# Input projection with 512-column matmuls for the high weights, ACT drains and an accumulating DMA

## The chip, the cores and the metric

The kernel runs on one core of one Trainium2 chip. The metric is the device time of one execution in microseconds; before the change it was 1963.8 us in the median of three runs (1961.78 to 1964.49). Five engines matter: PE multiplies matrices, DVE and ACT work elementwise (both read PE's result banks), POOL works elementwise between buffers of the on-chip memory, SP only issues transfers (DMAs). Each engine works off its own queue in order; between engines there are only semaphores.

## The reference, cut to what matters

The whole is a two-layer trunk in float32 over 512 positions of width 2048. The change touches one matrix product of the first layer, `h @ w_in`, 512 × 2048 by 2048 × 8192:

```python
def pool_mixer_layer(x, norm_g, w_in, w_group, scale, w_out):
    B, S, _ = x.shape
    h = rmsnorm(x, norm_g)
    proj = h @ w_in
    u, gate = proj[..., :W_A], proj[..., W_A:]
    ...
    y = y * jax.nn.silu(gate)
    return x + y @ w_out
```

Pooling over time, a product per group, the gate and an output product follow; then a shared key/value side, 16 heads of attention with a block-causal mask, and a last output product.

## The kernel before

Everything lies transposed: 128 channels on the partitions, 512 positions along a row. PE multiplies in a rounded 32-bit format. So that little precision is lost, each operand is split into a rounded high part and the low rest, and a product is three matmuls: high weight by high x, high weight by low x, low weight by high x.

The kernel is written for a framework that turns it into one instruction list for each engine: it allots buffers and adds semaphores, and orders the instructions by a timeline that it reckons beforehand. The order on each engine can therefore differ from the order of the text, but is fixed once built.

The input projection (lines 259 to 409) saves products with a scheme that does 2 × 2 blocks with seven products in place of eight. The blocks are two k-tiles of 128 (`2j`, `2j+1`), two output tiles (`pair`), and two halves of the positions, H = 256. There are NJ = 8 k-pairs `j`. The steps:

- An opening loop over `j` (lines 353 to 374) loads x, scales it with the norm's gain (`x_parts`, line 272), forms the seven combinations of x and splits them into `xh[j]` and `xl[j]`, which stay resident (`x_sums`, line 286). In the same loop four output tiles are computed without the scheme, to keep PE busy.
- Then come 30 pairs, in the order 18 to 31 and 0 to 15 (line 396), each with four rounds q of two k-pairs. In a round `w_combos` (line 294) loads the weights of the two output tiles into a `raw` buffer (three exist) with two DMAs of SP, forms four sums (two by one DVE addition, line 301; two by POOL, lines 303 and 304), has ACT round all seven into `hi` (line 307) and DVE subtract for `lo` (line 308). `hi` and `lo` have two buffers each.
- `seven` (line 318) issues the seven products of a k-pair, three matmuls of 256 columns each (lines 324, 326, 328). The seven sums of a pair lie in the halves of four banks, and there are two such sets (`banks`, line 311).
- `gather` (line 331) combines the seven sums into four blocks `e` straight out of the banks: one ACT copy (line 334) and four DVE additions (lines 335 to 338). The results go to scratch in HBM (line 347); pairs 0 to 3 pass through the first pooling beforehand (line 345).
- Beside the first pairs the squares of x for the norm are summed up (`square`, line 387): a load, an ACT square, a DVE addition each.

What comes after (pooling, the products of line 140 to 142 with 512 columns each, attention) is not changed.

Of the kernel before, what the change touches and what calls it, by code (L numbers as in the profile page):

```python
# [7 lines left out]
F32 = mybir.dt.float32  # L8
# [6 lines left out]
P = 128  # L15
S = 512
# [35 lines left out]
def trunk_kernel(  # L52
# [206 lines left out]
    with ExitStack() as c1:  # L259
        xcp = c1.enter_context(tc.tile_pool(name="xcp", bufs=NJ))  # L260
        w7 = c1.enter_context(tc.tile_pool(name="w7", bufs=2, **tile_))
        ps7 = c1.enter_context(tc.tile_pool(name="ps7", bufs=2, space=bass.MemoryType.PSUM))
        xh, xl = [None] * NJ, [None] * NJ

        def x_load(j):

# [4 lines left out]

        def x_parts(j, c, hp):

            h = xcp.tile([P, 7, H], F32R, tag="xh", name="xh")
            lo = xcp.tile([P, 7, H], F32R, tag="xl", name="xl")
            xh[j], xl[j] = h, lo
            h12 = hp.tile([P, H], F32R, tag="h12", name="h12", bufs=NJ)
            l12 = hp.tile([P, H], F32R, tag="l12", name="l12", bufs=NJ)
            A.activation(c[:, 2:8:5, :], c[:, 2:8:5, :], AF.Copy, scale=cs[:, C_GA + 2 * j:C_GA + 2 * j + 1])
            A.activation(c[:, 0:2, :], c[:, 0:2, :], AF.Copy, scale=cs[:, C_GA + 2 * j + 1:C_GA + 2 * j + 2])  # L280
            A.copy(h[:, 0:3, :], c[:, 0:3, :])
            V.tensor_tensor(lo[:, 0:3, :], c[:, 0:3, :], f(h[:, 0:3, :]), ALU.subtract)
            split(c[:, 7, :], h12, l12)
            return h12, l12

        def x_sums(j, c):
            h, lo = xh[j], xl[j]
            V.tensor_tensor(c[:, 3:5, :], c[:, 1:3, :], c[:, 7:8, :].broadcast_to([P, 2, H]), ALU.subtract)
            V.scalar_tensor_tensor(c[:, 5, :], c[:, 4, :], -1.0, c[:, 1, :], ALU.mult, ALU.subtract)
            V.scalar_tensor_tensor(c[:, 6, :], c[:, 5, :], -1.0, c[:, 0, :], ALU.mult, ALU.subtract)  # L290
            A.copy(h[:, 3:7, :], c[:, 3:7, :])
            V.tensor_tensor(lo[:, 3:7, :], c[:, 3:7, :], f(h[:, 3:7, :]), ALU.subtract)

        def w_combos(pair, q):

            c = w7.tile([P, 2, 8, P], F32, tag="raw", name="raw", bufs=3)
            for m in range(2):
                nc.sync.dma_start(c[:, :, 2 - 2 * m:4 - 2 * m, :],
                                  awin[2 * pair + m][:, q * S:(q + 1) * S].rearrange(
                                      "p (j k n) -> p j k n", j=2, k=2))  # L300
            V.tensor_tensor(c[:, :, 4:6, :], c[:, :, 0:1, :].broadcast_to([P, 2, 2, P]),  # L301
                            c[:, :, 1:3, :], ALU.add)
            G.tensor_tensor(c[:, :, 6, :], c[:, :, 4, :], c[:, :, 2, :], ALU.add)  # L303
            G.tensor_tensor(c[:, :, 7, :], c[:, :, 6, :], c[:, :, 3, :], ALU.add)
            hi = w7.tile([P, 2, 7, P], F32R, tag="hi", name="hi")
            lo = w7.tile([P, 2, 7, P], F32R, tag="lo", name="lo")
            A.copy(hi, c[:, :, 1:8, :])  # L307
            V.tensor_tensor(lo, c[:, :, 1:8, :], f(hi), ALU.subtract)  # L308
            return hi, lo

        def banks():
            return [ps7.tile([P, 2, H], F32, tag=f"k{i}", name=f"k{i}") for i in range(4)]


        SEVEN = ((2, 0, 0, 0), (0, 6, 1, 0), (1, 2, 2, 0), (3, 4, 3, 0),
                 (5, 5, 0, 1), (6, 1, 1, 1), (4, 3, 2, 1))

        def seven(ks, w, j):
            hi, lo = w
            for wi, xi, b, h in SEVEN:  # L320
                dst = ks[b][:, h, :]
                first, last = j == 0 and h == 0, j == NJ - 1

                T.matmul(dst, hi[:, j % 2, wi, :], xh[j][:, xi, :], start=first, stop=False,  # L324
                         skip_group_check=True)
                T.matmul(dst, hi[:, j % 2, wi, :], xl[j][:, xi, :], start=False, stop=False,  # L326
                         skip_group_check=True)
                T.matmul(dst, lo[:, j % 2, wi, :], xh[j][:, xi, :], start=False, stop=last,  # L328
                         skip_group_check=True)

        def gather(ks, pair):

            e = epool.tile([P, 7, H], F32, tag="e", name="e")
            A.copy(e[:, 6, :], ks[2][:, 0, :])
            V.tensor_tensor(e[:, 0:2, :], e[:, 6:7, :].broadcast_to([P, 2, H]), ks[0], ALU.add)
            V.tensor_tensor(e[:, 2, :], e[:, 1, :], ks[2][:, 1, :], ALU.add)
            V.tensor_tensor(e[:, 3:6:2, :], e[:, 1:3, :], ks[3][:, 0:1, :].broadcast_to([P, 2, H]), ALU.add)
            V.tensor_tensor(e[:, 4:7:2, :], e[:, 2:4, :], ks[1], ALU.add)
            for i, v in enumerate((e[:, 0:7:6, :], e[:, 4:6, :])):
# [10 lines left out]
        accs = [ps7.tile([P, 2, H], F32, tag=f"k{i}", name=f"k{i}") for i in range(4)]  # L350
        with ExitStack() as c2:
            hp = c2.enter_context(tc.tile_pool(name="hp", bufs=2, **tile_))
            for j in range(NJ):
# [11 lines left out]
                a, b = xh[j], xl[j]  # L365
# [11 lines left out]
        for o in range(0, 4, 2):  # L377
            e = epool.tile([P, 7, H], F32, tag="e", name="e")
            for i in range(2):
                v = e[:, 2 * i:2 * i + 2, :]  # L380
                A.copy(v, accs[o + i])
                raws[32 + o + i] = dram()
                nc.sync.dma_start(raws[32 + o + i].rearrange("p (h t) -> p h t", h=2), v)

        sq = [tt_(), tt_()]

# [7 lines left out]
                V.tensor_tensor(sq[k % 2], sq[k % 2], x, ALU.add)  # L394

        for n, pair in enumerate((*range(18, 32), *range(16))):
            ks = banks()
            for q in range(NJ // 2):
                w = w_combos(pair, q)
                seven(ks, w, 2 * q)  # L400
                seven(ks, w, 2 * q + 1)
            if n < 8:
                square(2 * n)
                square(2 * n + 1)
            if n == 8:
                V.tensor_tensor(sq[0], sq[0], sq[1], ALU.add)
                p = ps7.tile([P, 2, H], F32, tag="k3", name="k3").rearrange("p h t -> p (h t)")
# [528 lines left out]
```

## Time and profile before

| what | value |
|---|---|
| median of three runs | 1963.8 us |
| the profiled execution, whole | 1961.67 us |
| its span, first to last instruction | 1959.9 us |
| mean granted PE clock | 0.999 |
| ACT, DVE and POOL busy from 436 to 660 us | 78.3, 149.2, 71.2 of 224 us |
| mean DMA rate over the span | 120 GB/s |

A row of a group reads: line, engine, operation, written tile <- read tiles, shape, count | busy time, mean ns of one | idle time of the engine just before them, and what ended it. A row of the timeline begins with the start and the duration in microseconds. A matmul's duration there is longer than its share of PE's time, because matmuls are pipelined; the distance from one start to the next is what the stream pays. "k" are the banks of the input projection, "mm" those of the later products. The windows give busy time per engine in a stretch, then the granted clock, the mean busy share of the 16 DMA engines and GB/s. SPq is the queue of SP, from which the transfers are issued.

### The profile page before, as it was taken

To read this page: it belongs to the slowest core of one execution; us is meant where nothing else is said; L and a number is where in the kernel's file an instruction comes from. 1 tells how busy PE (TensorE), PEld (TensorE's weight loads), DVE (VectorE), ACT (ScalarE), POOL (GpSimd) and SP (SyncE) were. 2 spreads that over 40 slices of the span, in tenths; PEclk is the share of its full clock that TensorE was granted. 3 is DMA by queue.
4 is the path that set the end of the run, shared out by engine and by line. 5 is a ranking of instruction groups with operands and counts; after the bars stand their busy time and mean duration, and the time that the engine had idled before them with its cause. 6 is when DMAs were issued, how large, how long until landed. Compare 5 with 4: busy or idle time off the path is not lost.

```text
span 1959.9 us, 30545 instructions
## 1 busy us (share of the span) xinstructions
PE 1933.3 (99%) x11324; PEld 1707.0 (87%) x11324; DVE 1280.2 (65%) x2305; ACT 815.1 (42%) x1553; POOL 262.9 (13%) x404
## 2 busy tenths in 40 slices
PE   8999999999999999999999999999999999999999
PEld 7899999999999888888888888888888888878887
DVE  8766676797666587485694567573345888786432
ACT  7533333333333443333323454332245677774221
POOL 0432332334332100000000000000010111210000
PEclk9999999999999999999999999999999999999999
DMA  6644344435444464344344343233332111111632
GB/s 198 201 135 138 119 140 130 129 120 173 140 128 132 162 205 148 113 124 140 118 126 139 113 145 123 87 97 97 97 92 75 46 38 59 52 58 46 217 119 86
DMA packets 168134, 235.51 MB, mean 120 GB/s; under 512 B 14897, under 2 KB 95153, under 8 KB 167985
## 3 DMA queue, kind: packets, MB, share of 16 engines
q1 hardware_dynamic: 167696, 233.37, 37.9%
q8 instruction: 88, 1.44, 0.3%
q14 instruction: 62, 0.50, 0.1%
q10 hardware_dynamic: 288, 0.20, 0.0%
HBM read 208.35 MB, written 25.17 MB: 119 GB/s over the span
## 4 chain that ended last, share of the span: by engine, by line
PE 93%; DVE 3%; DMA 2%; issue 1%; ACT 1%; SPq 0%; DVEq 0%; ACTq 0%
PE mm L142 16%; PE mm L140 16%; PE mm L141 16%; PE k L328 9%; PE k L324 9%; PE k L326 9%; PE sc L728 3%; PE mm L604 1%; PE mm L602 1%; PE mm L603 1%; PE tr L687 1%; PE mm L622 1%; PE mm L624 1%; PE mm L623 1%; DVE lo L308 1%
## 5 line engine op out<-in xcount | busy, mean ns | idle before, releaser
L122 ACT CAST whi<-raw 128x512 fp32r<-128x512 f32 (+2 forms) x421 | 255.7, 611 | 518.9 <-PE mm L141 455.7
L324 PE MATMUL k<-xh,hi 128*128 128x256 f32 x1680 | 460.1, 283 | 0.1
L326 PE MATMUL k<-xl,hi 128*128 128x256 f32 x1680 | 460.0, 283 | 0.0
L123 DVE TENSOR_TENSOR wlo<-raw,whi 128x512 fp32r<-128x512 f32 (+2 forms) x421 | 281.9, 672 | 222.2 <-ACT whi L122 217.8
L328 PE MATMUL k<-xh,lo 128*128 128x256 f32 x1680 | 418.1, 284 | 3.9 <-DVE lo L308 3.9
L307 ACT CAST hi<-raw 128x1792 fp32r<-128x1792 f32 x120 | 202.8, 1690 | 373.5 <-PE k L328 258.2
L308 DVE TENSOR_TENSOR lo<-raw,hi 128x1792 fp32r<-128x1792 f32 x120 | 248.9, 2074 | 158.5 <-ACT hi L307 158.5
L142 PE MATMUL mm<-bt,wlo 128*128 128x512 f32 x860 | 335.3, 390 | 0.0
L140 PE MATMUL mm<-bt,whi 128*128 128x512 f32 x860 | 334.6, 389 | 0.0
L141 PE MATMUL mm<-bt,whi 128*128 128x512 f32 x860 | 334.4, 389 | 0.0
L324 PEld LDWEIGHTS k<-xh,hi 128*128 128x128 f32 x1680 | 322.5, 192 | 0.3 <-ACT hi L307 0.3
L326 PEld LDWEIGHTS k<-xl,hi 128*128 128x128 f32 x1680 | 322.5, 192 | 0.0
L328 PEld LDWEIGHTS k<-xh,lo 128*128 128x128 f32 x1680 | 296.7, 192 | 5.6 <-DVE lo L308 5.1
L140 PE MATMUL mm<-at,whi 128*128 128x512 f32 x516 | 201.7, 392 | 3.1 <-ACT whi L122 3.1
L142 PE MATMUL mm<-at,wlo 128*128 128x512 f32 x516 | 202.0, 392 | 2.2 <-DVE wlo L123 2.2
L141 PE MATMUL mm<-at,whi 128*128 128x512 f32 x516 | 201.8, 391 | 0.0
L142 PEld LDWEIGHTS mm<-bt,wlo 128*128 128x128 f32 x860 | 161.4, 188 | 34.3 <-issue 0.5
L140 PEld LDWEIGHTS mm<-bt,whi 128*128 128x128 f32 x860 | 161.4, 188 | 33.8 <-ACT whi L122 0.2
L141 PEld LDWEIGHTS mm<-bt,whi 128*128 128x128 f32 x860 | 161.4, 188 | 33.3
L303 POOL TENSOR_TENSOR raw<-raw 128x256 f32<-128x256 f32 x120 | 101.3, 844 | 437.3 <-DVE raw L301 414.7
L142 PEld LDWEIGHTS mm<-at,wlo 128*128 128x128 f32 x516 | 97.2, 188 | 24.1 <-DVE wlo L123 3.8
L140 PEld LDWEIGHTS mm<-at,whi 128*128 128x128 f32 x516 | 97.2, 189 | 23.6 <-ACT whi L122 3.7
(1152 smaller groups left out, 2573.4 us busy)
## 6 DMA issues: line engine op xcount, KB each, us to landing
raw<-awin SPq DMA_DIRECT2D x240, 256.0 KB, 3.2
raw<-awo SPq DMA_DIRECT2D x128, 256.0 KB, 2.8
raw<-bwin SPq DMA_DIRECT2D x80, 256.0 KB, 2.7
raw<-awg SPq DMA_DIRECT2D x64, 256.0 KB, 2.8
raw<-bwo SPq DMA_DIRECT2D x59, 256.0 KB, 2.8
scr<-e SPq DMA_DIRECT2D x56, 256.0 KB, 2.6
raw<-wkvb SPq DMA_DIRECT2D x32, 256.0 KB, 3.0
raw<-wqb SPq DMA_DIRECT2D x32, 192.0 KB, 2.4
```

What stands on the lines that cost most here:

```text
L122: A.copy(hi[:, :n], raw[:, :n])
L123: V.tensor_tensor(lo[:, :n], raw[:, :n], f(hi[:, :n]), ALU.subtract)
L140: T.matmul(dst, wh, xh, start=first, stop=False)
L141: T.matmul(dst, wh, xl, start=False, stop=False)
L142: T.matmul(dst, wl, xh, start=False, stop=last)
L303: G.tensor_tensor(c[:, :, 6, :], c[:, :, 4, :], c[:, :, 2, :], ALU.add)
L307: A.copy(hi, c[:, :, 1:8, :])
L308: V.tensor_tensor(lo, c[:, :, 1:8, :], f(hi), ALU.subtract)
L324: T.matmul(dst, hi[:, j % 2, wi, :], xh[j][:, xi, :], start=first, stop=False, skip_group_check=True)
L326: T.matmul(dst, hi[:, j % 2, wi, :], xl[j][:, xi, :], start=False, stop=False, skip_group_check=True)
L328: T.matmul(dst, lo[:, j % 2, wi, :], xh[j][:, xi, :], start=False, stop=last, skip_group_check=True)
L728: T.matmul(s[:, 0:n], l, r, start=(j == 0), stop=(j == 4))
```

## The change

- The high and the low part of each x combination now lie side by side in one tile `xc[j]`. A high weight tile is multiplied by both in one matmul of 512 columns, whose halves go to the halves of one bank; the low weight's matmul of 256 columns adds to the second half. A pair thus uses seven banks, of a pool of eight.
- The rounds run product by product, with both k-pairs inside. In the last round each bank is drained by an ACT copy of 512 columns into `e` once its product is finished; `gather` adds the halves with one DVE addition of 1792 elements a row and then combines with four more, all of it out of `e`. There is one `e` buffer in place of two.
- In `w_combos` the DVE addition goes. The half tile `a2[:, :, 0]` is loaded twice, into slots 4 and 5; two more loads fill slot 1 and slots 2 and 3 (four DMAs of SP in place of two, three of them in pieces of 512 bytes). One DMA issued by POOL then adds slots 1 and 2 to slots 4 and 5 within the on-chip memory. POOL's two sums, ACT's `hi` and DVE's `lo` follow as before.

```diff
-        ps7 = c1.enter_context(tc.tile_pool(name="ps7", bufs=2, space=bass.MemoryType.PSUM))
-        xh, xl = [None] * NJ, [None] * NJ
+        ps7 = c1.enter_context(tc.tile_pool(name="ps7", bufs=8, space=bass.MemoryType.PSUM))
+        xc = [None] * NJ
...
-            h = xcp.tile([P, 7, H], F32R, tag="xh", name="xh")
-            lo = xcp.tile([P, 7, H], F32R, tag="xl", name="xl")
-            xh[j], xl[j] = h, lo
+            xc[j] = xcp.tile([P, 7, 2, H], F32R, tag="xc", name="xc")
+            h, lo = xc[j][:, :, 0, :], xc[j][:, :, 1, :]
...
-            for m in range(2):
-                nc.sync.dma_start(c[:, :, 2 - 2 * m:4 - 2 * m, :],
-                                  awin[2 * pair + m][:, q * S:(q + 1) * S].rearrange(
-                                      "p (j k n) -> p j k n", j=2, k=2))
-            V.tensor_tensor(c[:, :, 4:6, :], c[:, :, 0:1, :].broadcast_to([P, 2, 2, P]),
-                            c[:, :, 1:3, :], ALU.add)
+            a1, a2 = (awin[2 * pair + m][:, q * S:(q + 1) * S].rearrange("p (j k n) -> p j k n", j=2, k=2)
+                      for m in range(2))
+            nc.sync.dma_start(c[:, :, 4, :], a2[:, :, 0, :])
+            nc.sync.dma_start(c[:, :, 5, :], a2[:, :, 0, :])
+            nc.sync.dma_start(c[:, :, 1, :], a2[:, :, 1, :])
+            nc.sync.dma_start(c[:, :, 2:4, :], a1)
+            nc.gpsimd.dma_start(c[:, :, 4:6, :], c[:, :, 1:3, :], accum_op=ALU.add)
...
+        PLACE = (1, 5, 0, 6, 2, 4, 3)
+
+        def seven(ks, w, q, e):
             hi, lo = w
-            for wi, xi, b, h in SEVEN:
...
+            for n, (wi, xi) in enumerate(SEVEN):
+                for i in range(2):
+                    x = xc[2 * q + i]
+                    T.matmul(ks[n], hi[:, i, wi, :], x[:, xi, :, :], start=q == 0 and i == 0, stop=False,
+                             skip_group_check=True)
+                    T.matmul(ks[n][:, 1, :], lo[:, i, wi, :], x[:, xi, 0, :], start=False,
+                             stop=q == NJ // 2 - 1 and i == 1, skip_group_check=True)
+                if q == NJ // 2 - 1:
+                    m = 2 * PLACE[n]
+                    A.copy(e[:, m:m + 2, :], ks[n])
+
+        def gather(e, pair):
+
+            V.tensor_tensor(e[:, 0:14:2, :], e[:, 0:14:2, :], e[:, 1:14:2, :], ALU.add)
+
+            V.tensor_tensor(e[:, 2:5:2, :], e[:, 0:1, :].broadcast_to([P, 2, H]), e[:, 2:5:2, :], ALU.add)
+            V.tensor_tensor(e[:, 6, :], e[:, 4, :], e[:, 6, :], ALU.add)
+            V.tensor_tensor(e[:, 0:14:13, :], e[:, 4:7:2, :], e[:, 12:13, :].broadcast_to([P, 2, H]), ALU.add)
+            V.tensor_tensor(e[:, 8:11:2, :], e[:, 0:7:6, :], e[:, 8:11:2, :], ALU.add)
+            for i, v in enumerate((e[:, 2:9:6, :], e[:, 10:14:3, :])):
...
-        epool = c1.enter_context(tc.tile_pool(name="epool", bufs=2, **tile_))
+        epool = c1.enter_context(tc.tile_pool(name="epool", bufs=1, **tile_))
...
         for n, pair in enumerate((*range(18, 32), *range(16))):
-            ks = banks()
+            ks = [bank() for _ in range(7)]
+            e = epool.tile([P, 14, H], F32, tag="e", name="e")
             for q in range(NJ // 2):
-                w = w_combos(pair, q)
-                seven(ks, w, 2 * q)
-                seven(ks, w, 2 * q + 1)
+                seven(ks, w_combos(pair, q), q, e)
...
-            gather(ks, pair)
+            gather(e, pair)
```

More of the change, by code (lines that the diff above doesn't have):

```diff
@@ L309, in w_combos @@
             return hi, lo
[L311 to L318, printed above, removed]
-            hi, lo = w
-            for wi, xi, b, h in SEVEN:
[L321 to L339, printed above, removed]
+        def bank():
+            return ps7.tile([P, 2, H], F32, tag="k", name="k")
@@ L347, in gather @@
                     nc.sync.dma_start(raws[o].rearrange("p (h t) -> p h t", h=2), v)
-        accs = [ps7.tile([P, 2, H], F32, tag=f"k{i}", name=f"k{i}") for i in range(4)]
+        accs = [bank() for i in range(4)]
         with ExitStack() as c2:
@@ L374, in trunk_kernel @@
                                  skip_group_check=True)
-        epool = c1.enter_context(tc.tile_pool(name="epool", bufs=2, **tile_))
+        epool = c1.enter_context(tc.tile_pool(name="epool", bufs=1, **tile_))
         tp[0] = c1.enter_context(tc.tile_pool(name="tpool1", bufs=6, **tile_))
[L377 to L383, printed above, removed]
+        e = epool.tile([P, 14, H], F32, tag="e", name="e")
+        for o in range(4):
+            v = e[:, 2 * o:2 * o + 2, :]
+            A.copy(v, accs[o])
+            raws[32 + o] = dram()
+            nc.sync.dma_start(raws[32 + o].rearrange("p (h t) -> p h t", h=2), v)
         sq = [tt_(), tt_()]
@@ L406, in trunk_kernel @@
                 V.tensor_tensor(sq[0], sq[0], sq[1], ALU.add)
[L407 removed]
+                p = bank().rearrange("p h t -> p (h t)")
                 ra[0] = norm_r(sq[0], D, p)
[L409 removed]
+            gather(e, pair)
     wpool = ctx.enter_context(tc.tile_pool(name="wpool", bufs=3, **tile_))
```

6 lines of the change are left out of this document (4 added, 2 removed).

## The prediction

> **What bounds the kernel now.** I read the page's engine shares and the chain that ended last first, then the windows of the stage that the change touches, then single instructions of each engine there.
>
> ```profile
> PE 1933.3 (99%) x11324; PEld 1707.0 (87%) x11324; DVE 1280.2 (65%) x2305; ACT 815.1 (42%) x1553; POOL 262.9 (13%) x404
> PE 93%; DVE 3%; DMA 2%; issue 1%; ACT 1%; SPq 0%; DVEq 0%; ACTq 0%
> core 0: us, PE busy (x) PEld busy (x) DVE busy (x) ACT busy (x) POOL busy (x), PEclk, DMA share, GB/s
> 44.00:92.00 48.00, 44.28 (x336) 41.91 (x335) 35.55 (x36) 27.20 (x32) 21.54 (x17) 1.00 0.62 198
> 260.00:400.00 140.00, 140.00 (x1169) 140.00 (x1169) 98.43 (x97) 48.08 (x36) 44.13 (x60) 1.00 0.41 129
> 436.00:660.00 224.00, 224.00 (x1869) 223.98 (x1868) 149.15 (x140) 78.27 (x56) 71.23 (x89) 1.00 0.45 141
> ```
>
> TensorE sets the end. In the input projection it is busy without a gap from 92 us on at full clock, and only the first 48 us show idle time (48.00 − 44.28 = 3.7 us). So time is won here only by asking less of PE, and lost as soon as anything feeds it more slowly than it works. What one product costs PE is the distance between starts, not the pipelined duration (the second column):
>
> ```profile
> 502.05 0.28 PE L324 MATMUL k<-xh,hi 128*128 128x256 f32 x1
> 502.17 0.28 PE L326 MATMUL k<-xl,hi 128*128 128x256 f32 x1
> 502.29 0.28 PE L328 MATMUL k<-xh,lo 128*128 128x256 f32 x1
> L324 PE MATMUL k<-xh,hi 128*128 128x256 f32 x1680 | 460.1, 283 | 0.1
> ...
> 999.79 0.39 PE L140 MATMUL mm<-bt,whi 128*128 128x512 f32 x1
> ...
> 1005.91 0.39 PE L140 MATMUL mm<-bt,whi 128*128 128x512 f32 x1
> ...
> 47.83 0.39 PE L371 MATMUL k<-xh,hi 128*128 128x512 f32 x1
> ...
> 49.23 0.39 PE L371 MATMUL k<-xh,hi 128*128 128x512 f32 x1
> ```
>
> A matmul of 256 columns takes 0.120 us of the stream; one of 512 takes 0.2267 us (999.79 to 1005.91 are 27 of them in a row). One q, two k-tiles of 42 matmuls together, is therefore 42 × 0.120 = 5.04 us, and 30 pairs × 4 q = 120 q make 604.8 us.
>
> **PE after the change.** The 1680 products keep their L328 matmul, and L324 and L326 become one of 512 columns: 0.2267 instead of 0.240, so 0.0133 us each, 1680 × 0.0133 = **22.4 us less**. One q becomes 14 × (0.2267 + 0.120) = 4.853 us, a pair 19.41. Both widths already stand mixed in the opening phase: 47.83 to 49.23 holds three of 512 and six of 256 columns, and 3 × 0.2267 + 6 × 0.120 = 1.40 us is what it took, so the mixture costs nothing. This gain holds only while each q's weights are ready every 4.853 us, so the rest is about those.
>
> **What feeds PE.** The three `raw` buffers go round: load, sums, `hi`, `lo`, free again. One turn before:
>
> ```profile
> 304.17 1.69 ACT L307 CAST hi<-raw 128x1792 fp32r<-128x1792 f32 x1 [3.35 <-PE k L328]
> 305.89 2.02 DVE L308 TENSOR_TENSOR lo<-raw,hi 128x1792 fp32r<-128x1792 f32 x1 [2.41 <-ACT hi L307]
> 307.94 0.88 SPq L298 DMA_DIRECT2D raw<-awin  x2
> DMA to landing us min/median/max: 2.7/3.2/4.7
> 307.83 0.68 DVE L301 TENSOR_TENSOR raw<-raw 128x512 f32<-128x512 f32 x1
> 313.70 0.73 POOL L303 TENSOR_TENSOR raw<-raw 128x256 f32<-128x256 f32 x1 [3.49 <-DVE raw L301]
> 314.51 0.74 POOL L304 TENSOR_TENSOR raw<-raw 128x256 f32<-128x256 f32 x1
> ```
>
> `hi` and `lo` from 304.17 to 307.91 are 3.74 us; SP then issues two loads 0.51 us apart (0.88 − 0.37), the second landing 0.51 + 3.2 = 3.7 us later; the DVE sum is 0.68, the POOL sums 313.70 to 315.25 are 1.55; I allow 0.3 for the hand-overs, estimated from the gaps of some 0.05 between such rows. That is 10.0 us for a buffer, 3.3 us per q with three buffers, against the 5.04 that PE wants: 5.1 us of a turn's 15.1 are waiting, which is the ACT row's idle time (it waits for PE to give back a `hi` buffer).
>
> After: four loads, the fourth issued 3 × 0.51 = 1.5 us after the first, landing at 4.7; the DVE sum goes; the accumulating DMA comes in with a time A from issue to landing: 3.74 + 4.7 + A + 1.55 + 0.3 = **10.3 + A**. PE's new pace allows 3 × 4.853 = 14.56, so the gain is whole up to **A = 4.3 us**, and eaten up at 3 × 5.04 = 15.12, **A = 4.8 us**. Beyond, each microsecond costs 120 / 3 = 40 us.
>
> The trace of before holds no DMA from POOL, none within SBUF and none that adds. The nearest rows:
>
> ```profile
> dsp<-xt SPq DMA_DIRECT2D x16, 256.0 KB, 2.1
> scr<-e SPq DMA_DIRECT2D x56, 256.0 KB, 2.6
> xt<-dsp SPq DMA_DIRECT2D x16, 256.0 KB, 4.8
> 92.00:228.00 136.00, 136.00 (x1134) 136.00 (x1135) 89.21 (x85) 46.59 (x34) 42.85 (x56) 1.00 0.43 134
> 760.00:1200.00 440.00, 440.00 (x1943) 364.34 (x1942) 287.27 (x456) 165.79 (x274) 1.78 (x16) 1.00 0.42 130
> ```
>
> Lower end 2.1 us, a plain 256 KB read out of SBUF. Upper end 6.5: the 4.8 of loads that wait in a crowd, and as much again for the second operand as the doubled packets below. I take **A = 4.0**: the store in 1 KB pieces, the same size and cut, 2.6; plus 0.85 because the old sums must be read as well (16 packets an engine at 53 ns: share 0.43 of 16 engines over 134 GB/s is 53 ns per 1 KB); plus some 0.55 for POOL's issue, a little over SP's distance of 0.51. The ring is then 14.3 us, 4.77 per q: under PE's 4.853, but by only 0.26 us a turn. The Trainium skill, DMA: Bandwidth & Descriptors, section "Anatomy of one DMA — SWDGE (gpsimd) path", fits a DMA issued from GpSimd as 2.0 us plus the bytes over 436 GB/s; for this size that is 2.6 us, and by it the ring would be 12.9 us, 4.3 per q; no run here shows it yet, and the fit is for a plain copy.
>
> **The DMA engines.** Packets of 1 KB take 53 ns, and by the same working the 2 KB packets of the 760:1200 row 106 ns, so time goes with bytes. The 512-byte pieces of the three half loads therefore cost 27 ns if this holds on, 53 at worst. Per q and engine: now 0.43 × 5.04 = 2.17 us; the loads change from 16 packets of 1 KB to 16 of 1 KB and 48 of 512 B, +0.45 (at 27; 48 × 27 − 16 × 53) to +1.7 us; the accumulation adds 0.85 to 1.7. Sum 3.5 to 5.6 us of 4.853; by the nearer rows 3.5 to 4.3, 72 to 89%. The cover holds, but loads will land later than 3.2 us at times.
>
> **ACT and DVE.** The rows for what is added and removed:
>
> ```profile
> 57.13 0.58 ACT L381 COPY e<-k 128x512 f32<-128x512 f32 x1
> L334 ACT COPY e<-k 128x256 f32<-128x256 f32 x30 | 10.9, 364 | 8.4 <-PE k L328 8.4
> L308 DVE TENSOR_TENSOR lo<-raw,hi 128x1792 fp32r<-128x1792 f32 x120 | 248.9, 2074 | 158.5 <-ACT hi L307 158.5
> 309.15 0.42 DVE L336 TENSOR_TENSOR e<-e,k 128x256 f32<-128x256 f32 x1
> 309.60 0.69 DVE L337 TENSOR_TENSOR e<-e,k 128x512 f32<-128x512 f32 x1
> 310.32 0.69 DVE L338 TENSOR_TENSOR e<-e,k 128x512 f32<-128x512 f32 x1
> ```
>
> ACT per pair: 4 × 1.69 + 0.36 = 7.1 us now; 4 × 1.69 + 7 × 0.58 = 10.8 of 19.41 after. DVE per pair: 4 × (2.07 + 0.68) + 2.5 for the gather (0.68, 0.42, 0.69, 0.69) = 13.5 now; after, four `lo` of 2.07, an addition as long as one `lo` (1792 elements) and the same 2.5: 12.8. Neither becomes the bound. But the gather is now 4.5 us in one piece at the pair's end, after the last drain. Drains follow products 0.69 us apart, each frees its bank 0.58 later, and with eight banks the next pair asks for the first reused one a q later: hidden. If all of the gather stands ahead of a `lo` on DVE, that `lo` and the release of its buffer are up to 4.5 us late, with `hi` matmuls of a q (14 × 0.2267 = 3.2 us) as cover ahead of the first `lo` matmul. Bounds 0 to 1.3 us a pair; I take 0.1, **+3 us** over 30, because in the rows around 309 the gather already stands ahead of a `lo` and PE lost nothing. SP gets two issues more a q: 4 × 0.51 = 2.0 of 4.85 us, covered; stores queue behind them for nobody's loss. POOL's queue holds its two sums behind the DMA's wait for four loads; only the ring waits for them, and it is counted there. The opening phase's other tile layout and the last drains cost nothing that a row shows.
>
> **The opening.**
>
> ```profile
> L324 PE MATMUL k<-xh,hi x1680: 277/283/384, 55.5 to 666.6; 128*128 128x256 f32 x187
> 666.97 0.13 PE k L328
> ```
>
> From 55.5 us, where the first of the products stands, to the last at 667.1 are 611.6 us, 6.8 more than 604.8, all before 92 us, where the squares and their loads (DMA share 0.62) crowd the ring. Some 7 q there are 2.3 turns, each longer by 4.0 + 1.0 − 0.68 = 4.3 us: +10 if nothing covers it, 0 if it hides in the waits for squares. I take **+5**.
>
> **Sum.** The profiled execution took 1961.7 us in all (span 1959.9), 2.1 below the median of the three runs, 1963.8. 1961.7 − 22.4 + 3 + 5 = 1947.3; between this and the same from the median (1949.4) I predict **1948**. Its own range is 1938 (no loss at all, 1939.3, less about what runs differ by) to 1957 (the opening at +10 and some 8 at the pairs' ends).
>
> **Rivals.**
>
> **The accumulating DMA paces the stage (slower).** Place: the ring of three buffers. At A = 5.5 the turn is 15.8, 5.27 per q: 120 × 0.23 = +27 and +5 at the opening, **1994**; it decides from A = 4.8. For it: 0.26 us of margin, and later landings in a busier queue act like A. Against it: plain transfers out of SBUF at 2.1 to 2.6.
>
> **POOL's sums meet DVE.** They now start when a DMA lands, not when DVE has just finished.
>
> ```profile
> L304 POOL TENSOR_TENSOR raw<-raw x60: 735/742/2414, 98.2 to 395.8; 128x256 f32<-128x256 f32 x60
> ```
>
> A sum that collides takes 2.41 instead of 0.74 us. One such a turn makes it 16.0, 5.32 per q: +34 and +5, **2000**; in half of the turns it is 5.04, **1967**. The median of 742 speaks against it as things stand, DVE's 66% load for it. The Trainium skill, SBUF — State Buffer, section "Who interferes with whom", states this rule: a DVE instruction with two SBUF inputs shares a read port with GpSimd, and the later one waits until the other is done; the 2414 ns agree (2.03 of `lo` and more).
>
> **The DMA engines fill up.** 5.6 us per q at the upper prices: +64, **2030**. The 2 KB and 1 KB rows speak against it.
>
> **Nothing measurable.** Losses at the opening and the pairs' ends add up to the 22 us, **1963**.
>
> **Chances.** Forecast 0.55; the DMA paces 0.19; POOL meets DVE 0.13 (0.03 of it near 1967, within 0.2%); DMA engines full 0.06; nothing measurable 0.07. About 0.2% (4 us) is what a measurement here can tell from no change: faster 0.55, same 0.10, slower 0.35. The range runs from 1938 to 1998: it leaves out the full DMA engines, the worst collisions and the upper end of A.
>
> **What would show it.** Right: `k` matmuls with 512 columns at 0.227 us, starts of q 4.85 us apart from 92 us on, ACT's `hi` still idle for PE. Wrong: PE idle before `hi` or `lo` matmuls, `hi` waiting for POOL, POOL waiting for its DMA, turns over 14.6 us; POOL sums near 2.4 us with DVE's `lo` beside them name the second rival, a DMA share above 0.95 the third.

## The result and the profile after

The changed kernel takes **2113.84 us** (median of 4 runs, 2110.9 to 2116.22) beside 1962.79 us for the kernel before in the same session (4 runs, 1960.97 to 1964.49): a ratio of 1.0767, 95% interval 1.0754 to 1.0781, so 151 us slower where 1948 us had been forecast. The profiled execution took 2116.2 us with a span of 2114.4.

From the page of the changed kernel: the busy time of the engines, the chain that ended last, and three of its costliest groups (busy time and mean ns of one, then the idle time before them and its releaser).

```profile
PE 1987.5 (94%) x9644; PEld 1625.3 (77%) x9644; DVE 1282.0 (61%) x2215; ACT 909.2 (43%) x1733; POOL 447.7 (21%) x524
...
PE 61%; DMA 18%; DVE 6%; POOL 4%; ACT 4%; issue 3%; SPq 3%; POOLq 0%; DVEq 0%; ACTq 0%
...
L307 ACT CAST hi<-raw 128x1792 fp32r<-128x1792 f32 x120 | 202.2, 1691 | 444.9 <-POOL raw L304 304.1
...
L303 POOL TENSOR_TENSOR raw<-raw 128x256 f32<-128x256 f32 x120 | 132.4, 1103 | 313.0 <-DMA raw<-raw 312.8
...
L302 POOL DMA_DIRECT2D raw<-raw x120 | 143.8, 1203 | 102.1 <-DVE lo L146 45.2
```

TensorE was 93% of the chain before and is 61% now; DMA went from 2% to 18%. The `hi` cast on ACT used to idle for PE; now it idles for POOL's second weight sum, and POOL's first weight sum (L303) idles 313 us for the accumulating DMA within `raw`. The windows of the projection (the first number is the length, then the busy time of PE, of PEld, which is PE's loading of weights, of DVE, ACT and POOL, the granted clock, the DMA share and GB/s) show the loss spread over the whole stage:

```profile
92.00:228.00 136.00, 116.60 (x616) 95.26 (x615) 77.55 (x60) 57.57 (x64) 67.81 (x65) 0.97 0.76 174
228.00:436.00 208.00, 178.01 (x916) 143.58 (x915) 113.62 (x85) 81.36 (x88) 107.70 (x98) 0.95 0.71 166
436.00:660.00 224.00, 192.59 (x957) 148.21 (x956) 136.07 (x110) 89.64 (x98) 115.11 (x112) 0.98 0.71 166
```

PE has some 14% of idle time in each, where it had none; no engine is full, and the DMA engines are at 0.71 to 0.76. So something is passed round one after the other. The view of the `k` tile's matmuls (shortest, median and longest in ns, then the first and the last start) bounds the stage, and the timeline of PE shows the distance between starts:

```profile
L326 PE MATMUL k<-xc,hi x1680: 387/395/796, 55.0 to 821.9; 128*128 128x512 f32 x187
L328 PE MATMUL k<-xc,lo x1680: 274/280/681, 56.4 to 822.1; 128*128 128x256 f32 x187
```

```profile
404.67 0.40 PE L326 MATMUL k<-xc,hi 128*128 128x512 f32 x1
404.91 0.40 PE L328 MATMUL k<-xc,lo 128*128 128x256 f32 x2
405.14 0.39 PE L326 MATMUL k<-xc,hi 128*128 128x512 f32 x1
```

From 404.67 to 405.14 lie one matmul of 512 and two of 256 columns in 0.47 us: 0.2267 + 2 × 0.120, as forecast. PE's own gain is there. But the stage lasts 822.1 − 55.0 = 767 us, 6.39 us a q, where PE needs 4.853 and the kernel before took 611.6 / 120 = 5.10. The timeline of POOL in the changed kernel shows what a q waits for (start, length, and in brackets the idle time before it with its releaser):

```profile
405.21 1.20 POOL L302 DMA_DIRECT2D raw<-raw  x1 [0.73 <-issue]
411.32 0.73 POOL L303 TENSOR_TENSOR raw<-raw 128x256 f32<-128x256 f32 x1 [4.91 <-DMA raw<-raw]
412.12 0.73 POOL L304 TENSOR_TENSOR raw<-raw 128x256 f32<-128x256 f32 x1
412.79 1.19 POOL L302 DMA_DIRECT2D raw<-raw  x1
414.21 1.20 POOL L302 DMA_DIRECT2D raw<-raw  x1 [0.22 <-issue]
417.12 0.72 POOL L303 TENSOR_TENSOR raw<-raw 128x256 f32<-128x256 f32 x1 [1.72 <-DMA raw<-raw]
417.92 0.74 POOL L304 TENSOR_TENSOR raw<-raw 128x256 f32<-128x256 f32 x1
418.62 2.52 POOL L303 TENSOR_TENSOR raw<-raw 128x256 f32<-128x256 f32 x1
421.22 2.40 POOL L304 TENSOR_TENSOR raw<-raw 128x256 f32<-128x256 f32 x1
```

POOL issues a q's DMA, stands 4.91 us until it lands, does the two sums, and only then (412.79, with no idle time ahead) issues the next q's DMA. Now and then two DMAs go out together (412.79 and 414.21). The last two rows show something else: sums of 2.52 and 2.40 us in place of 0.73. DVE works from on-chip memory at that time:

```profile
418.01 2.52 DVE L336 TENSOR_TENSOR e<-e 128x1792 f32<-128x1792 f32 x1 [1.39 <-ACT e L332]
420.46 2.56 DVE L308 TENSOR_TENSOR lo<-raw,hi 128x1792 fp32r<-128x1792 f32 x1
```

**Theory 1 (POOL's order):** POOL works its queue in order, so the next q's DMA stands behind this q's sums, and these behind this q's DMA; a q takes a whole trip through POOL. **Rivals:** the ring of three buffers with a slow DMA; the DMA engines; POOL's sums meeting DVE; and, for what is not the DMA, the drains by ACT into one tile.

### The profile page after: what moved, and what is told of

Read it like the earlier page. It is cut to its first block, busy times and chain, and to the rows that moved or that the text cites. A ratio compares the mean times of both kernels' runs of the same rounds, so it can differ in the third digit from the quotient of the medians.

```text
span 2114.4 us, 27942 instructions
## 1 busy us (share of the span) xinstructions
PE 1987.5 (94%) x9644; PEld 1625.3 (77%) x9644; DVE 1282.0 (61%) x2215; ACT 909.2 (43%) x1733; POOL 447.7 (21%) x524
## 3 DMA queue, kind: packets, MB, share of 16 engines
q0 software_dynamic: 32640, 31.46, 10.0%
## 4 chain that ended last, share of the span: by engine, by line
PE 61%; DMA 18%; DVE 6%; POOL 4%; ACT 4%; issue 3%; SPq 3%; POOLq 0%; DVEq 0%; ACTq 0%
PE mm L140 15%; PE mm L142 15%; PE mm L141 15%; DMA raw<-raw 11%; DMA raw<-awin 6%; DVE lo L308 4%; PE sc L729 3%; POOL raw L303 3%; ACT hi L307 3%; POOL raw L304 1%; PE mm L603 1%; PE mm L604 1%; PE mm L605 1%; PE k L326 1%; SPq L299 1%
## 5 line engine op out<-in xcount | busy, mean ns | idle before, releaser
L326 PE MATMUL k<-xc,hi 128*128 128x512 f32 x1680 | 587.0, 411 | 87.1 <-ACT hi L307 85.1
L326 PEld LDWEIGHTS k<-xc,hi 128*128 128x128 f32 x1680 | 317.2, 193 | 163.3 <-ACT hi L307 107.0
L308 DVE TENSOR_TENSOR lo<-raw,hi 128x1792 fp32r<-128x1792 f32 x120 | 248.8, 2074 | 311.9 <-ACT hi L307 264.4
L328 PE MATMUL k<-xc,lo 128*128 128x256 f32 x1680 | 388.9, 291 | 18.1 <-DVE lo L308 16.4
L328 PEld LDWEIGHTS k<-xc,lo 128*128 128x128 f32 x1680 | 325.1, 194 | 79.9 <-DVE lo L308 49.4
L303 POOL TENSOR_TENSOR raw<-raw 128x256 f32<-128x256 f32 x120 | 132.4, 1103 | 313.0 <-DMA raw<-raw 312.8
L302 POOL DMA_DIRECT2D raw<-raw x120 | 143.8, 1203 | 102.1 <-DVE lo L146 45.2
L304 POOL TENSOR_TENSOR raw<-raw 128x256 f32<-128x256 f32 x120 | 120.2, 1002 | 9.3
```

Source lines behind the costliest of these rows:

```text
L302: nc.gpsimd.dma_start(c[:, :, 4:6, :], c[:, :, 1:3, :], accum_op=ALU.add)
L326: T.matmul(ks[n], hi[:, i, wi, :], x[:, xi, :, :], start=q == 0 and i == 0, stop=False, skip_group_check=True)
L328: T.matmul(ks[n][:, 1, :], lo[:, i, wi, :], x[:, xi, 0, :], start=False, stop=q == NJ // 2 - 1 and i == 1, skip_group_check=True)
```

## The experiments

Times with a ratio are medians of four or seven runs; the others are of one run each. The kernel before took 1962.1 to 1963.8 us beside them throughout. The expectations call some runs by a label, which stands in brackets behind the heading.

### The two halves of the change

**One half: wide matmuls and drains, with the weight sum back on DVE (e1).** The changed kernel with the loads and the DVE addition of before.

```diff
-            nc.sync.dma_start(c[:, :, 4, :], a2[:, :, 0, :])
...
-            nc.gpsimd.dma_start(c[:, :, 4:6, :], c[:, :, 1:3, :], accum_op=ALU.add)
...
+            V.tensor_tensor(c[:, :, 4:6, :], c[:, :, 0:1, :].broadcast_to([P, 2, 2, P]),
+                            c[:, :, 1:3, :], ALU.add)
```

> The changed kernel with the two whole loads and the DVE addition of before put back; the 512-column matmuls, the seven banks with their ACT drains and the new gather stay. If the way of the weights (the ring of three raw buffers, POOL's queue, or full DMA engines) is what costs, PE gets its new pace of 4.85 us a q and the time is 1940 to 1950 us. If the PE part itself is at fault (drains, banks, the long gather), it stays well above 1963 us.

Measured 2008.05 us, ratio 1.0227 (1.021 to 1.0244): a miss. Without any accumulating DMA this half alone costs 45 us. So the change holds two faults, and this one is taken up below.

**The other half: the kernel before with four loads and the accumulating DMA (e2).**

```diff
-            V.tensor_tensor(c[:, :, 4:6, :], c[:, :, 0:1, :].broadcast_to([P, 2, 2, P]),
-                            c[:, :, 1:3, :], ALU.add)
...
+            nc.gpsimd.dma_start(c[:, :, 4:6, :], c[:, :, 1:3, :], accum_op=ALU.add)
```

> The kernel of before with only the four loads and the accumulating DMA in place of two loads and the DVE addition; matmuls of 256 columns as before. If the way of the weights costs, q come some 6.2 to 6.4 us apart as in the changed kernel whatever PE asks, 2095 to 2125 us. If the PE part costs, about 1965 us.

Measured 2092.78 us, +130, just below the range named for the way of the weights: this half is most of the loss. The two add up to 175, more than the 151 of both, so the first half costs less beside this one. From 100 to 660 us `lo` takes 2074 ns on average in the changed kernel and 2226 in the first half alone; which of the changes between them does that wasn't tested.

**The four loads alone**, DVE adding.

```diff
-            nc.gpsimd.dma_start(c[:, :, 4:6, :], c[:, :, 1:3, :], accum_op=ALU.add)
+            V.tensor_tensor(c[:, :, 4:6, :], c[:, :, 4:6, :], c[:, :, 1:3, :], ALU.add)
```

> The kernel of before with the four loads of the change (the half tile twice), and the DVE addition of before taking its first operand from the doubled slots; no accumulating DMA. All theories of the weights' way: the turn of a raw buffer grows by about 1 to 2 us to 11 to 12 us, far under 15.1, so no change, 1960 to 1966 us. It shows how late the fourth load lands. Well above 1970 us would put part of the cost on the loads themselves.

Measured 1962.31 us: the two more loads a q and their 512-byte pieces cost nothing.

### The accumulating DMA: ring, engines, addition or order

**The addition left out of the DMA.**

```diff
-            nc.gpsimd.dma_start(c[:, :, 4:6, :], c[:, :, 1:3, :], accum_op=ALU.add)
+            nc.gpsimd.dma_start(c[:, :, 4:6, :], c[:, :, 1:3, :])
```

> The changed kernel with POOL's DMA as a plain copy of slots 1 and 2 to slots 4 and 5; the addition is left out. Its packets should take about half as long (some 50 in place of 102 ns per 1 KB), 0.8 us less from issue to landing. Ring theory: 0.8 / 3 = 0.27 us a q, 32 us less, about 2080 us. POOL-queue theory: 0.8 us in the three of four q that stand one behind the other, 70 us less, about 2040 us. If only the adding makes the DMA slow, 1950 us.

Measured 2065.4 us. From the pages, first of the changed kernel, then of this one: the queue from POOL (packets, MB, share of 16 engines) and the DMA's size and time from issue to landing:

```profile
q0 software_dynamic: 32640, 31.46, 10.0%
...
raw<-raw POOLq DMA_DIRECT2D x120, 256.0 KB, 4.6
```

```profile
L302 POOL DMA_DIRECT2D raw<-raw x120 | 86.8, 724 | 155.5 <-DMA raw<-awin 80.3
...
raw<-raw POOLq DMA_DIRECT2D x120, 256.0 KB, 3.7
```

The adding makes the landing 0.9 us later and POOL's issue 1203 ns instead of 724, and is worth 48 us of the 151. A plain copy still loses 103, in which the first half's fault (45 when alone) is contained: the addition is a part of the loss and not the whole of it. The time lies between what the ring (2080) and the order on POOL (2040) were said to give, so this run doesn't separate those two.

**A fourth raw buffer in the second half (e7)** (room made by one `h12`/`l12` less and four instead of six square tiles).

```diff
-            c = w7.tile([P, 2, 8, P], F32, tag="raw", name="raw", bufs=3)
+            c = w7.tile([P, 2, 8, P], F32, tag="raw", name="raw", bufs=4)
```

> The kernel of before with four loads and accumulating DMA (as e2) and four raw buffers in place of three; to make room, one buffer less for the opening's halves and four instead of six small tiles. If the ring of buffers is the limit, a turn of 18.4 us over four buffers is 4.6 us a q, PE's 5.04 binds again: 1962 to 1975 us. If POOL's queue is the limit, whose order in this kernel is strictly DMA, sum, sum, DMA, each q takes 1.2 + 4.5 + 1.5 = 7.2 us whatever the buffers: 2180 to 2230 us. If the DMA engines are full, 2090 us as e2.

Measured 2103.17 us, outside all three ranges: the ring theory falls, since a third more room in the ring brought nothing. By its size the time is nearest to the one named for full DMA engines, 2090; the next run decides on those. POOL's timeline and POOL's waits (100 to 700 us; us in total, times, longest) of this kernel:

```profile
402.14 1.19 POOL L303 DMA_DIRECT2D raw<-raw  x1
406.75 0.74 POOL L304 TENSOR_TENSOR raw<-raw 128x256 f32<-128x256 f32 x1 [3.42 <-DMA raw<-raw]
407.57 0.74 POOL L305 TENSOR_TENSOR raw<-raw 128x256 f32<-128x256 f32 x1
408.24 1.20 POOL L303 DMA_DIRECT2D raw<-raw  x1
```

```profile
POOL raw L304 <- DMA raw<-raw: 330.3, 96, 5.1
POOL raw L303 <- issue: 0.9, 3, 0.5
POOL raw L303 <- DMA raw<-awin: 0.5, 3, 0.2
```

A period of 408.24 − 402.14 = 6.10 us: issue 1.19, idle 3.42, two sums. The DMA itself waits for its loads 0.5 us in 600: they have long landed. It waits only for its place in the queue. 120 × 6.10 = 732 us, and the stage lasts 745 (800.7 − 55.5 by the view of the `k` tile). The size of 2180 to 2230 that the order theory had named was too large, because the 4.6 us of the landing already contain the 1.2 us of the issue.

**The order turned:** with four buffers, the next q's DMA is issued on POOL ahead of this q's sums.

```diff
+        def w_next():
+            c, _ = ahead.pop(0)
+            ahead.append(w_load(*todo.pop(0)) if todo else (None, None))
+            return w_combos(c, ahead[0][1])
...
+            with tc.issue_after(behind.ins) if behind else ExitStack():
+                G.tensor_tensor(c[:, :, 6, :], c[:, :, 4, :], c[:, :, 2, :], ALU.add)
```

> e7 (kernel of before with four loads, accumulating DMA, four raw buffers) with one thing changed: on POOL the accumulating DMA of the next q is issued ahead of the two sums of this q. If POOL's queue is the limit (in e7 one q takes 1.2 us of issue, 3.4 to 4.5 of waiting and 1.5 of sums one behind the other), PE's 5.04 us binds again: 1962 to 1985 us. If the DMA engines (0.72 busy) or the DMA's latency in itself are the limit, 2085 to 2105 us as e7.

Measured **1974.98 us**: 128 of the 140 us that the run before lost come back with no instruction changed, only its place. The loads of the next q move ahead together with their DMA, but it had waited for them for 0.5 us only. POOL's waits (100 to 690 us) and the window of the steady stage:

```profile
POOL raw L308 <- DMA raw<-raw: 9.9, 15, 1.9
```

```profile
436.00:660.00 224.00, 223.29 (x1859) 222.88 (x1858) 134.06 (x97) 78.32 (x56) 176.56 (x136) 1.00 0.87 205
```

The sums wait 9.9 us for the DMA instead of 330, and PE is full again (223.3 of 224) at a DMA share of 0.87. So **POOL's order is the cause** of what this half loses, and the DMA engines are not, though they are near their end.

**The same order in the changed kernel**, with its three buffers (the edit as above).

> The changed kernel with POOL's order turned round in the same way (next q's DMA ahead of this q's sums) and its three raw buffers kept. POOL-queue theory: most of the 150 us goes; what stays is the ring of three, 3.7 + 5.3 + 4.7 + 1.6 + 0.3 = 15.6 us or 5.2 us a q, and the PE part's own loss: 1980 to 2015 us. If the order doesn't matter, 2100 to 2120 us.

Measured 2172.05 us, slower still: both expectations missed. POOL's DMA group (100 to 660 us) in this kernel:

```profile
L302 POOL DMA_DIRECT2D raw<-raw x82 | 98.5, 1201 | 297.0 <-DMA raw<-awin 150.1 <-DVE lo L312 105.7 <-issue 23.7
```

Now the DMA waits, 297 us in all, for its loads and for the `lo` that frees its buffer, and this q's sums stand behind it. With three buffers the next q's buffer is that of q − 2, so two q share one trip: casts 3.74, loads of some 5.3, issue 1.2, sums of some 2.0, hand-overs 0.3, an estimate of 12.5 us or 6.3 a q; measured are (878.2 − 55.4) / 120 = 6.86 by the view of the `k` tile, so it accounts for most of it. With four it would be three q to a trip, 4.2. The order needs the fourth buffer: with it the run before was fast, and in the last run below, a changed kernel with four, POOL's DMA waits 161 us in place of these 297. That run differs in its drains too, so the buffer alone wasn't isolated.

**POOL's two sums moved to DVE**, so that POOL's queue holds DMAs alone.

```diff
-            G.tensor_tensor(c[:, :, 6, :], c[:, :, 4, :], c[:, :, 2, :], ALU.add)
-            G.tensor_tensor(c[:, :, 7, :], c[:, :, 6, :], c[:, :, 3, :], ALU.add)
+            V.tensor_tensor(c[:, :, 6, :], c[:, :, 4, :], c[:, :, 2, :], ALU.add)
+            V.tensor_tensor(c[:, :, 7, :], c[:, :, 6, :], c[:, :, 3, :], ALU.add)
```

> The changed kernel with the two POOL sums moved to DVE, so that nothing on POOL stands between one accumulating DMA and the next. If POOL's queue is the limit (the next q's DMA held behind the sums of this one, which wait for this one's DMA), PE gets its pace: 1945 to 1960 us. If the ring of three buffers is the limit, a turn is 3.7 for hi and lo, 5.7 for the loads, 5.8 for the DMA, 0.9 for the sums and 0.3, 16.4 us or 5.5 us a q: 2005 to 2035 us. If the DMA engines are the limit, no change, 2100 to 2120 us.

Measured 2186.82 us, a miss for all, the theory of POOL's order too. From the page of this kernel, and from the waits of PE's weight loads (100 to 660 us):

```profile
L303 DVE TENSOR_TENSOR raw<-raw 128x256 f32<-128x256 f32 x120 | 50.9, 424 | 320.4 <-DMA raw<-raw 302.0
```

```profile
PEld k L328 <- DVE lo L308: 116.6, 44, 6.3
```

The same wait, 302 us, has moved to DVE's queue, where `lo` parts stand behind these sums, and PE waits for `lo`. This is read from the waits; no further run tested it. In the two forms the engine that consumes the DMA's result carries the wait.

### What the wide matmuls' half loses

**The sum of halves in a tile of its own**, so that ACT's drains needn't wait for it or the stores (weight sum on DVE, as in the first run).

```diff
-            V.tensor_tensor(e[:, 0:14:2, :], e[:, 0:14:2, :], e[:, 1:14:2, :], ALU.add)
...
+            e = epool.tile([P, 8, H], F32, tag="s", name="s")
+            V.tensor_tensor(e[:, 0:7, :], d[:, 0:14:2, :], d[:, 1:14:2, :], ALU.add)
```

> e1 (512-column matmuls, ACT drains, DVE weight sum) with the sum of the halves written to a tile of its own, so that the drained tile is free again after the first of the five gather additions and not after the stores have landed; four small tiles instead of six. If the single drained tile is what costs in e1 (its drains wait for the stores of the pair before), PE gets its pace: 1945 to 1960 us. If DVE's longer gather and its collisions with POOL's sums cost, 1990 to 2010 us.

Measured 2001.32 us, in the range named for DVE's load and collisions: some 7 of 45, so the single tile is a small part.

**POOL's two sums left out** of the first run (zeros are written in their place).

```diff
-            G.tensor_tensor(c[:, :, 6, :], c[:, :, 4, :], c[:, :, 2, :], ALU.add)
-            G.tensor_tensor(c[:, :, 7, :], c[:, :, 6, :], c[:, :, 3, :], ALU.add)
+            G.memset(c[:, :, 6:8, :], 0.0)
```

> e1 with POOL's two weight sums left out: POOL writes zeros into their slots instead, so it reads nothing. If e1's loss comes from DVE and POOL getting in each other's way (lo at 2.23 in place of 2.07, POOL's sums at 1.2 to 1.5 in place of 0.8 us), lo goes back to 2.02 and PE to its pace: 1940 to 1960 us. If DVE is simply given too much work in too long pieces (the gather of 4.5 us ahead of lo), only the collisions' part of DVE's time, some 0.3 us a q, goes: 1980 to 2000 us.

Measured 1963.45 us, between the two expectations: 45 us gone. The groups of DVE and POOL from 100 to 660 us, first with the sums, then without:

```profile
L307 DVE TENSOR_TENSOR lo<-raw,hi 128x1792 fp32r<-128x1792 f32 x102 | 227.0, 2226 | 19.6 <-ACT hi L306 19.5
...
L335 DVE TENSOR_TENSOR e<-e 128x1792 f32<-128x1792 f32 x25 | 61.8, 2470 | 0.1
...
L303 POOL TENSOR_TENSOR raw<-raw 128x256 f32<-128x256 f32 x103 | 149.5, 1452 | 7.8
```

```profile
L306 DVE TENSOR_TENSOR lo<-raw,hi 128x1792 fp32r<-128x1792 f32 x110 | 222.3, 2021 | 36.3 <-ACT hi L305 36.1
...
L334 DVE TENSOR_TENSOR e<-e 128x1792 f32<-128x1792 f32 x28 | 56.5, 2019 | 0.2 <-ACT e L330 0.2
```

With POOL reading, `lo` takes 2226 ns on average instead of 2021, the sum of halves 2470 instead of 2019, and POOL's own sum 1452, twice its undisturbed 735. In the first run PE's weight loads then wait for `lo` and for the drained tile, and hardly for `hi` (100 to 660 us):

```profile
PEld k L327 <- DVE lo L307: 38.8, 42, 2.6
PEld k L325 <- ACT e L331: 21.1, 16, 2.9
PEld k L325 <- ACT hi L306: 1.8, 2, 1.5
```

Without POOL's reads the first two are 10.8 and 6.1 us. A rival would be that two sums less ahead of `hi` merely make the weights' way shorter; with 1.8 us of waiting for `hi` there was little to win by that.

**Half of a bank drained by ACT, the other half added by DVE from the bank (e9)**, with two drained tiles.

```diff
-                    A.copy(e[:, m:m + 2, :], ks[n])
+                    A.copy(e[:, m, :], ks[n][:, 0, :])
+                    V.tensor_tensor(e[:, m, :], e[:, m, :], ks[n][:, 1, :], ALU.add)
```

> e1 with another closing: ACT copies only the first half of each bank (256 columns), DVE adds the second half straight out of the bank, and the result has half the columns, so that two result tiles fit. No wait for stores, and the halves' addition has one operand in a bank instead of two in the on-chip memory. Single-tile theory: 1945 to 1960 us. Collision theory: the halves no longer collide with POOL, four shorter additions still do, 1960 to 1990 us. If DVE's load decides (16.5 of 19.4 us a pair), 1980 us or more.

Measured 1979.26 us, ratio 1.008 (1.0063 to 1.0097): the better form of this half, with fewer DVE reads from on-chip memory, but slower than before all the same. The time lies in the range of the collision theory and at the edge of that for DVE's load, so it doesn't separate these two.

**That form with the DVE weight sum on POOL.**

```diff
-            V.tensor_tensor(c[:, :, 4:6, :], c[:, :, 0:1, :].broadcast_to([P, 2, 2, P]),
+            G.tensor_tensor(c[:, :, 4:6, :], c[:, :, 0:1, :].broadcast_to([P, 2, 2, P]),
```

> e9 (halves added out of the banks) with the weight sum of two slots moved from DVE to POOL, which then forms all four. DVE gets 0.7 us a q back. If DVE's load is what is left of e9's loss: 1940 to 1965 us. If collisions are, POOL's doubled reads collide more: 1975 to 2010 us.

Measured 1971.52 us, between the two ranges and 8 below the form before. DVE has less to do but collides more: `lo` takes 2491 ns on average, and POOL is busy for 506 of the 560 us from 100 to 660.

**POOL's sums left out of the two best forms of this half**, as above (zeros in their place).

> The changed kernel with the DVE addition for the weights, the halves' sum in a tile of its own, and POOL's two weight sums left out (zeros are written in their place). Question: why the changed matmuls without POOL's reads took 1963 and not 1945. Theory, the drained tile: ACT's drains stand waiting for the stores of the one drained tile; with the sum in its own tile that wait goes at each pair's end: 1945 to 1955. Rival, the opening and the first pairs (squares, loads, few ready weights) hold what is left: 1958 to 1966.

Measured 1957.42 us, ratio 0.9971 (0.996 to 0.9982), between the two ranges: 6 us below the run with the single drained tile, 44 below its own form with POOL's reads.

> The changed kernel with the DVE addition for the weights, each bank drained as a half by ACT and a half added by DVE from the bank, two drained tiles, and POOL's two weight sums left out (zeros are written in their place). With POOL's reads this form took 1979. Theory, collisions of DVE and POOL hold nearly all that this form loses: 1945 to 1955. Rival, the opening and the first pairs: 1958 to 1966. Third, DVE's seven additions a pair stand ahead of lo parts: 1965 to 1980 in spite of no reads by POOL.

Measured 1954.81 us, ratio 0.9955 (0.9938 to 0.9972), in the range of the collision theory: 24 us below the form with reads. So where DVE and POOL don't meet, the wide matmuls are some 9 us ahead of the kernel before, of the 22. That kernel wasn't run without POOL's reads, but has little to win by it, since PE is full in its windows from 92 us on. The windows of this run up to 100 us and after it:

```profile
44.00:100.00 56.00, 53.23 (x306) 45.57 (x305) 42.05 (x54) 34.00 (x46) 5.79 (x11) 1.00 0.62 198
100.00:660.00 560.00, 551.11 (x3127) 476.92 (x3127) 443.22 (x574) 256.53 (x306) 57.52 (x116) 1.00 0.44 133
```

After 100 us PE still idles for some 9 us of 560, so the opening isn't all that is left. The weight loads' waits in the same stretch name `lo` with 12.2 us; DVE is busy for 443 of 560 us. How the rest divides between the two wasn't measured.

**All remedies together:** accumulating DMA, four buffers, the order turned, banks drained in halves.

> The whole change in a form that takes up what the runs showed: accumulating DMA, four raw buffers, the next q's DMA on POOL ahead of this q's sums, each bank drained as a half by ACT and a half added by DVE from the bank, two drained tiles of eight columns blocks. Question: do the parts' prices add up, or does the DMA, which takes the weight sum off DVE, also take collisions away? Adding up: before 1963 + 12 (the accumulating DMA in this order) + 16 (wide matmuls with halves drained) = 1985 to 1995. Collisions go with DVE's load (485 of 560 us busy before, some 420 here): 1963 + 12 - 9 (what the wide matmuls give without POOL's reads) = 1960 to 1970. The DMA engines (share 0.87 at 5.04 us a q, so some 0.90 to 0.93 at 4.85) fill up: above 2000.

Measured 1993.36 us, ratio 1.0159 (1.0142 to 1.0176), in the range for prices that add up. The groups of POOL's sums and of `lo` (100 to 660 us):

```profile
L307 POOL TENSOR_TENSOR raw<-raw 128x256 f32<-128x256 f32 x107 | 146.1, 1365 | 19.8 <-DMA raw<-raw 19.6
L308 POOL TENSOR_TENSOR raw<-raw 128x256 f32<-128x256 f32 x106 | 136.4, 1287 | 8.2
```

```profile
L312 DVE TENSOR_TENSOR lo<-raw,hi 128x1792 fp32r<-128x1792 f32 x105 | 233.6, 2232 | 103.1 <-ACT hi L311 97.4 <-PE k L332 4.7 <-DMA raw<-awin 0.9
```

The wait for the DMA is gone (19.6 us), but the collisions stay: `lo` at 2232 ns, the sums at 1.3 us. Taking the weight sum off DVE didn't take them away. Longer instructions alone don't decide the time, though. In the run that turned the order, with 256-column matmuls, `lo` was as long while PE was full, and DVE had twice the idle time ahead of `lo`; in this run POOL's second sum holds up `hi`, `hi` holds up `lo`, and PE waits for `lo` (100 to 660 us, the first row of that run, the others of this one):

```profile
L313 DVE TENSOR_TENSOR lo<-raw,hi 128x1792 fp32r<-128x1792 f32 x109 | 244.5, 2244 | 196.7 <-ACT hi L312 150.2 <-DMA raw<-awin 46.2
```

```profile
ACT hi L311 <- POOL raw L308: 177.0, 69, 4.5
PEld k L332 <- DVE lo L312: 35.5, 36, 2.4
```

How the 31 us divide between the longer sums and POOL's trip, in which the next DMA's wait for its inputs now stands ahead of the sums, isn't shown. No version with the whole computation was faster than the kernel before.

## Why the prediction was wrong, step by step

**The step that failed:** "POOL's queue holds its two sums behind the DMA's wait for four loads; only the ring waits for them, and it is counted there." What stands behind the sums wasn't asked: the next q's DMA. The prediction's own numbers would have given it: A of 4.0 and sums of 1.55 are 5.55 us for one q's trip through POOL, above PE's 4.853, so 120 × (5.55 − 5.04) = 61 us slower than before, not 14 faster. Measured were 6.10 us in the kernel before with the DMA and four buffers, and 1975 us once the order was turned. The ring, on which both the forecast and the first rival rested, wasn't the bound in that order: a fourth buffer alone gave nothing (in the changed kernel it wasn't tried alone). The signs that the prediction had named for being wrong came: `hi` idles 304 us for POOL, and POOL 313 us for its DMA. The first rival had the right part (the DMA paces the stage) with the wrong place and so a price of 1994.

**PE's gain of 22.4 us: right** as a pitch (0.47 us for one wide and two narrow matmuls), but given only where weights come in time; without POOL's reads some 9 of it reached the end.

**A = 4.0: too small by 0.6**, within its bounds. At 4.6 the ring is 14.9 us, 4.97 a q, so by the prediction's own sum, with +3 and +5, the time would have been 1961 us, about that of before and not 151 above it. The Trainium skill, DMA: Bandwidth & Descriptors, section "Anatomy of one DMA — SWDGE (gpsimd) path", gives an estimate of 2.6 us for this size by its fit. Here the plain copy landed at 3.7 and the accumulating one at 4.6, so in this kernel the measurements decide against the fit.

**Loads at nothing: right** (1962.31). **DMA engines, 3.5 to 4.3 us a q, 72 to 89%: a little low.** With the order turned, the share of 0.87 at 5.04 us a q is 4.4 us, which would be 90% of 4.853; PE was full all the same. The accumulation, put at 0.85 to 1.7 us an engine and q, is 0.100 × 16 × 2114.4 us / 32640 = 104 ns a packet, 17 packets an engine, 1.76 us, just above its upper bound.

**Pairs' ends at +3 us: mis-sized.** The term treated the gather as work that stands ahead of a `lo`. It has become 1792 elements read twice from on-chip memory, where before one operand came from a bank, and POOL reads there too. That is the second rival, "POOL's sums meet DVE", and for this half alone it is what happened (2008 us, 1963 without POOL's reads). That its price of 2000 lies near is luck: it was worked out from the ring with the accumulating DMA in it, which this half doesn't have, and what is held up here is `lo` and the drained tile. The row held against it, a median of 742 ns, came from a kernel in which POOL's sums start as DVE falls idle for `hi`; this half takes that idle time away (`lo` idles 158 us for `hi` from 100 to 660 us before, 19.5 here), so the row couldn't speak for the kernel after. The Trainium skill, SBUF — State Buffer, section "Who interferes with whom", states that a DVE instruction with two SBUF inputs contends with a GpSimd instruction that reads SBUF. The runs agree: `lo` is 205 ns longer on average and the sums are twice as long.

**The opening at +5 us: not separated.** PE's busy time from 44 to 92 us fell from 44.28 to 40.57 us, but the 14% that PE idles in the later windows would already be 6.7 us of these 48, so the window says nothing of the opening by itself.

The slow cases were priced by the ring, by collisions or by full DMA engines (2030, outside the range that ended at 1998), and none by the order of one engine's queue.

## What to carry to other kernels

Where an engine both issues a DMA and consumes what it brings, add up one whole trip in its queue, issue, landing and use, and compare it with the pace that is wanted; here more buffers didn't help until the next issue was put ahead of the present use, and that order in turn needed the extra buffer. When work is moved between DVE, POOL and ACT, ask of each instruction whether its inputs lie in on-chip memory or in a bank, and what POOL reads meanwhile: a median duration from a trace in which two engines seldom met says little of a kernel in which they do.

## What the runs showed of the hardware

An accumulating DMA within on-chip memory costs more than a copy of the same bytes in three places: POOL's issue is 1203 ns against 724, the landing 4.6 us against 3.7, and the time on the engines 10.0% of the span for 31.46 MB in 32640 packets. The copy's 31.46 MB went in fewer and larger packets and took less than half of that; how much of it is the adding and how much the size of the packets isn't separated:

```profile
q0 software_dynamic: 9600, 31.46, 4.2%
```

A sum on POOL that meets DVE took 2.40 to 2.52 us instead of 0.73, and DVE paid as well, with 2.52 and 2.56 us for instructions that take 2.02 without POOL's reads. The granted clock of PE was 0.95 to 0.98 in the windows of the changed kernel's stage, where PE idles for 14%, and 1.00 in those of the kernel before. Pauses alone don't settle it: the run with four buffers had 1.00 from 92 to 436 us with PE idle for 12 to 13%. Why wasn't looked into.
